# First mixer of a seven-stage transformer kernel: three pieces of the norm per weight tile, the rotation's addition in halves, the maxima of heads 8 to 15 scaled on ScalarE

## The chip, the cores and the metric

The kernel runs on one core of a Trainium2 chip. The metric is device time in microseconds (us) of one execution, as a median over runs. The core has five engines that run their own instruction lists and meet by semaphores: TensorE (PE; its weight loads are PEld), VectorE (DVE), ScalarE (ACT), GpSimd (POOL) and SyncE (SP), which issues the weight loads from memory.

## The reference, cut to what matters

The input has 256 rows of 1024 columns. The program is a chain of seven stages: a feed-forward (`f1`), an attention mixer (`m1`), `f2`, a second mixer (`ab`), `f3`, a third (`cd`), `f4`. All of it is in float32. Only `m1` matters here:

```python
h = _rmsnorm(x, mix_pre_g[l])
qkv = h @ w_qkv[l]
qa, ka, va, qb, kb, vb = jnp.split(qkv, QKV_SPLITS, axis=-1)
qa = _rmsnorm(qa.reshape(B, S, N_HEADS_A, HEAD_DIM), q_norm_g[l])
ka = _rmsnorm(ka.reshape(B, S, N_KV_A, HEAD_DIM), k_norm_g[l])
...
qa = _apply_axial_rope(qa, ang_row, ang_col)
ka = _apply_axial_rope(ka, ang_row, ang_col)
out_a = _gqa_dense_blocked(qa, ka, va)
qb = _apply_rope(qb.reshape(B, S, N_HEADS_B, HEAD_DIM), ang_1d)
kb = _apply_rope(kb.reshape(B, S, N_HEADS_B, HEAD_DIM), ang_1d)
out_b = _dilated_mixture(qb, kb, vb)
heads = jnp.concatenate([out_a.reshape(B, S, A_Q), out_b.reshape(B, S, B_QKV)], axis=-1)
x = x + _rmsnorm(heads @ w_out[l], mix_post_g[l])
```

Heads 0 to 7 (group a) have a norm per head and dense attention over 256 keys; heads 8 to 15 (group b) have a mask (`c_maskb`, which adds up the three dilated patterns) and no norm. Each head is a softmax of 256 x 256 logits.

## The kernel before

Every float32 matmul operand is split into a high and a low part, and a product takes three matmuls (`mm3`). Weights stream in tiles of 128 x 1024: SP loads `wraw`, ACT casts it to the high part `wh` (line 89), DVE (in a few places POOL) subtracts to get the low part `wl` (line 94). There are 4 raw and 6 split buffers; a tile is split about six tiles ahead of its use.

In `m1` the projections come first. `gemm_a` (line 559) takes four weight tiles; after each it runs `self.pump(2)`, that is two small functions from the list `self.bg`, and then perhaps a function of `between`. The first `gemm_a` has in `self.bg` the nine pieces of `rope_a` (norm and rotation: the queries of rows 128 to 255, then the two keys' halves); the second transposes the rotated heads (`tr`, line 810) and runs `step(0)`; the third has the eight pieces of `rope_b` (rotation of the group-b queries and keys) in `self.bg`, and runs `step(1)` to `step(4)` after its four tiles. Then `step(5)` to `step(19)` follow without a projection.

A step is a slot of a software pipeline over the 16 heads, written out in this order: `logits(i)` (six matmuls `lg`, then row maxima `mx` on DVE, for heads 8 to 15 by two instructions of line 848 that add the mask as well, then the scaling of `mx` by -0.125 at line 850), `soft(i-1)` (two exponentials on ACT with `mx` as bias, a reciprocal on DVE at line 859, a product on POOL at line 860), in even steps `pair` (ACT and DVE write out two heads), `trans(i-3)` (four transposes `pT`, ACT's cast to `pp` at line 870, DVE's subtraction for the low part of `pp` at line 871), `pv_(i-4)` (six matmuls `o`, of which the last two read the low part of `pp`). From step 16 on, a piece of the output projection (`wo`) stands in the place of the logits. The tiles `t3` of the rotation and `pp` of the steps come from the same two buffers (tag `pp`).

Nothing is scheduled by a compiler: each engine's list has the order in which the code was written, and an engine takes its list from the front.

Of the kernel before, what the change touches and what calls it, by code (L numbers as in the profile page):

```python
# [11 lines left out]
AF = mybir.ActivationFunctionType  # L12
ALU = mybir.AluOpType
# [175 lines left out]
class Kern:  # L189
# [366 lines left out]
            self.pump(1)  # L556
        return pv

    def gemm_a(self, between=None):

        bank = [self.ps("ga0"), self.ps("ga1")]
        for i in range(4):
            wh, wl = self.ws.take(1)[0]
            for h in range(2):
                t = slice(h * P, (h + 1) * P)
                prods = [((self.xh[:, 2 * i + k, t], self.xl[:, 2 * i + k, t]), (wh[:, k, :], wl[:, k, :]))
                         for k in range(2)]
                self.mm3(bank[h], prods, i == 0, i == 3)
            self.pump(2)
            if between and i in between:  # L570
                between[i]()
        return bank
# [148 lines left out]
    def mixer1(self, gnext):  # L721
        nc, A = self.nc, self.A
        tt = nc.vector.tensor_tensor
        with ExitStack() as st:
# [8 lines left out]
            rb = T([P, 2, 16, 64], "rb")  # L733
# [5 lines left out]
                out=fl(qa[:, h, 0:8, :]), in_=self.gemm_a_half(h, mid, sf)))  # L739
# [47 lines left out]
            def rope_b(h):  # L787
                w = {}

                def a():  # L790
                    w["t"] = ap.tile([P, 16, 64], F32, name="t3", tag="pp", bufs=2)
                    tt(out=rb[:, h], in0=qb[:, h], in1=rope[:, h, 2:3, :].to_broadcast([P, 16, 64]), op=ALU.mult)

                def b(y):
                    a, b = slice(32 * y, 32 * y + 32), slice(32 - 32 * y, 64 - 32 * y)
                    tt(out=w["t"][:, :, a], in0=qb[:, h, :, b],
                       in1=rope[:, h, 3:4, a].to_broadcast([P, 16, 32]), op=ALU.mult)

                def c():
                    tt(out=rb[:, h], in0=rb[:, h], in1=w["t"], op=ALU.add)  # L800

                return [a, lambda: b(0), lambda: b(1), c]

            def tr(src, dst, chunks):

                for c in chunks:
                    p = self.ps("tq")
                    for j, cc in enumerate(c):
                        for h in range(2):
                            nc.tensor.transpose(p[:, j * S + h * P:j * S + (h + 1) * P],  # L810
                                                src[:, h, cc * P:(cc + 1) * P], self.ident)
                    n = len(c)
                    pv = p[:, :n * S].rearrange("p (a t) -> p a t", a=n)
                    hi, lo = (t[:, c[0]:c[-1] + 1:max(1, c[-1] - c[0]), :] for t in dst)
                    nc.scalar.copy(out=hi, in_=pv)
                    tt(out=lo, in0=pv, in1=hi.bitcast(F32), op=ALU.subtract)
# [10 lines left out]
            def logits(i):  # L827
                p = self.ps("lg")
                pv = p.rearrange("p (h k) -> p h k", h=2)
                if i < 8:  # L830
                    o = 64 * (i // 4)
                    q, k = [t[o:o + 64, i % 4, :] for t in qta], [t[o:o + 64, 4, :] for t in qta]
                else:
                    n = i - 8
                    o = 64 * (n % 2)
                    q, k = [t[o:o + 64, n // 2, :] for t in qtb], [t[o:o + 64, 4 + n // 2, :] for t in qtb]
                for h in range(2):
                    t = slice(h * P, (h + 1) * P)
                    self.mm3(pv[:, h, :], [((q[0][:, t], q[1][:, t]), k)], True, True)
                mx = self.sm.tile([P, 2], F32, name="mx", tag="mx")  # L840
                e = ap.tile([P, 2, S], F32, name="e", tag="e")
                if i < 8:
                    src = pv
                    nc.vector.tensor_reduce(out=mx, in_=pv, axis=AX.X, op=ALU.max)
                else:
                    src = e
                    for h in range(2):
                        nc.vector.tensor_tensor_reduce(out=src[:, h, :], in0=pv[:, h, :], in1=mask[:, h, :], scale=1.0,
                                                       scalar=-3e38, op0=ALU.add, op1=ALU.max, accum_out=mx[:, h:h + 1])
                nc.vector.tensor_scalar(out=mx, in0=mx, scalar1=-0.125, scalar2=None, op0=ALU.mult)  # L850
                lg[i] = src, e, mx

            def soft(i):
                src, e, nm = lg[i]
                l = self.sm.tile([P, 2], F32, name="ls", tag="ls")
                for h in range(2):
                    nc.scalar.activation(out=e[:, h, :], in_=src[:, h, :], func=AF.Exp, bias=nm[:, h:h + 1], scale=0.125,
                                         accum_out=l[:, h:h + 1])
                nc.vector.reciprocal(out=l, in_=l)
                nc.gpsimd.tensor_tensor(out=e, in0=e, in1=l.rearrange("p (h o) -> p h o", o=1).to_broadcast([P, 2, S]),  # L860
                                        op=ALU.mult)

            def trans(i):
                e = lg.pop(i)[1]
                p = self.ps("pT")
                for k in range(2):
                    for h in range(2):
                        nc.tensor.transpose(p[:, k * S + h * P:k * S + (h + 1) * P], e[:, h, k * P:(k + 1) * P], self.ident)
                t = ap.tile([P, 2, 512], F32R, name="pp", tag="pp", bufs=2)
                nc.scalar.copy(out=t[:, 0, :], in_=p)  # L870
                tt(out=t[:, 1, :], in0=p, in1=t[:, 0, :].bitcast(F32), op=ALU.subtract)
                pt[i] = t

            def pv_(i):
                pp = pt.pop(i).rearrange("p x (k q) -> p x k q", k=2)
                c = i // 2
                if i % 2 == 0:
                    od[c] = self.ps("o")[:, 0:256]
                o = od[c]
                prods = []  # L880
                for k in range(2):
                    o1 = 2 * (i // 4) + 1 - i % 2 if i < 8 else i % 2
                    v = [(t[:, k] if i < 8 else t[:, k, c - 4])[:, o1:o1 + 2, :].rearrange("p a w -> p (a w)")
                         for t in (va if i < 8 else vb)]
                    prods.append((v, (pp[:, 0, k, :], pp[:, 1, k, :])))
                ops = [(v[0], p[0]) for v, p in prods] + [(v[1], p[0]) for v, p in prods] + [(v[0], p[1]) for v, p in prods]
                for n, (v, p) in enumerate(ops):
                    nc.tensor.matmul(out=o, lhsT=v, rhs=p, start=i % 2 == 0 and n == 0, stop=i % 2 == 1 and n == 5)  # L888

            def pair(c):  # L890
                o = od.pop(c)
                hi, lo = heads(c)
                nc.scalar.copy(out=hi, in_=o)
                tt(out=lo, in0=o, in1=hi.bitcast(F32), op=ALU.subtract)
# [12 lines left out]
            def step(i):  # L907
                if i < 16:
                    logits(i)
                else:  # L910
                    wout(i - 16, 0)
                if 1 <= i < 17:
                    soft(i - 1)
                if i >= 6 and i % 2 == 0:
                    pair((i - 6) // 2)
                if 3 <= i < 19:
                    trans(i - 3)
                if i >= 4:
                    pv_(i - 4)
                if i == 5:  # L920
                    qtb.extend([mp.tile([P, 8, S], F32R, name="qtbh", tag="qb"), mp.tile([P, 8, S], F32R, name="qtbl")])
                if 5 <= i < 9:
                    tr(rbf, qtb, ((i - 5, i - 1),))
                if i in (8, 10, 12, 14):
                    self.ws.copy_next()(nc.gpsimd)


            bank = self.gemm_a()
            for h in range(2):
                nc.scalar.copy(out=fl(qb[:, h, 0:8, :]), in_=bank[h])  # L930
            self.flush()
            bank = self.gemm_a({1: lambda: tr(raf, qta, ((4,), (0, 1))), 2: lambda: tr(raf, qta, ((2, 3),)), 3: lambda: step(0)})
            for h in range(2):
                nc.scalar.copy(out=fl(qb[:, h, 8:16, :]), in_=bank[h])
            self.bg += rope_b(0) + rope_b(1)
            bank = self.gemm_a({i: lambda i=i: step(i + 1) for i in range(4)})
            self.ws.used()
            for h in range(2):
                hi, lo = (t[:, h, :, 0:3:2, :] for t in vb)
# [831 lines left out]
```

## Time and profile before

| | us |
|---|---|
| median of 3 runs (1093.35 to 1094.99) | 1094.9 |
| the profiled execution | 1095.59 |
| its span, first to last instruction | 1093.8 |
| PE busy in the span | 1077.5 (99%) |
| DVE busy | 737.9 (67%) |
| ACT busy | 597.6 (55%) |
| POOL busy | 314.9 (29%) |

The span is what the trace shows, 1.8 us less than the execution's time. Matmuls are pipelined, so a PE that is busy by the table may still be short of its peak. Shares are means over stages with different limits.

### The profile page before, as it was taken

The numbers are of one execution on the slowest core, as the hardware profiler recorded it, in microseconds if no ns is written. First come the engines' busy times: TensorE is split into PE (matmuls) and PEld (weight loads), VectorE is DVE, ScalarE is ACT, GpSimd is POOL, SyncE is SP. The second block draws the span as 40 slices with busy tenths as digits, with TensorE's granted clock in tenths as the row PEclk, the third lists the DMA queues.
The fourth block names the chain that finished last, engine by engine and source line by source line (L and its number), as shares of the span: only waits on it lengthen the run. The fifth ranks groups of instructions, "written<-read, shape, count | busy, mean of one in ns | idle before, by whom it ended". The sixth has DMA issues, their size and how long they took to land.

```text
span 1093.8 us, 16124 instructions
## 1 busy us (share of the span) xinstructions
PE 1077.5 (99%) x5963; PEld 921.9 (84%) x5963; DVE 737.9 (67%) x1023; ACT 597.6 (55%) x952; POOL 314.9 (29%) x564
## 2 busy tenths in 40 slices
PE   8999999999999999999999999999999999999997
PEld 5888888878878888888988888888889888888886
DVE  5665676889676655657775676766778567565564
ACT  4567555556656555556576554554553465554553
POOL 4005840213310000004014699999406100000000
PEclk9999999999999999999999999999999999999999
DMA  7765665672057555655624665565554346656651
GB/s 249 244 209 174 194 209 175 184 220 78 20 158 228 196 190 192 195 190 174 216 77 132 208 198 174 168 200 186 162 177 159 96 135 204 201 171 203 203 171 61
DMA packets 130256, 190.83 MB, mean 174 GB/s; under 512 B 6017, under 2 KB 101249, under 8 KB 130178
## 3 DMA queue, kind: packets, MB, share of 16 engines
q1 hardware_dynamic: 129440, 187.72, 53.7%
q0 software_dynamic: 736, 2.08, 0.7%
q8 instruction: 47, 0.77, 0.3%
q14 instruction: 31, 0.25, 0.1%
q10 hardware_dynamic: 2, 0.00, 0.0%
HBM read 188.73 MB, written 1.05 MB: 174 GB/s over the span
## 4 chain that ended last, share of the span: by engine, by line
PE 89%; DVE 5%; ACT 1%; issue 1%; POOL 1%; DMA 1%; SPq 0%; POOLq 0%; DVEq 0%; ACTq 0%
PE gb L535 27%; PE f L523 21%; PE gb L537 13%; PE wo L523 5%; PE gb L523 5%; PE fh L642 4%; PE gh L523 3%; PE ga L523 2%; DVE wl L94 1%; PE tp L370 1%; PE lg L523 1%; PE o L888 1%; PE M L1392 1%; DMA wraw<-in_w_first_dram 1%; DMA wraw<-in_w_qkv_dram 1%
## 5 line engine op out<-in xcount | busy, mean ns | idle before, releaser
L94 DVE TENSOR_TENSOR wl<-wraw,wh 128x1024 fp32r<-128x1024 f32 x338 | 411.5, 1258 | 107.1 <-ACT wh L89 106.0
L535 PE MATMUL gb<-xt,wh 128*128 128x512 f32 x1280 | 439.3, 390 | 0.0
L89 ACT CAST wh<-wraw 128x1024 fp32r<-128x1024 f32 x340 | 344.8, 1049 | 54.3 <-PE f L523 11.0
L537 PE MATMUL gb<-xt,wl 128*128 128x256 f32 x1280 | 354.0, 277 | 0.0
L535 PEld LDWEIGHTS gb<-xt,wh 128*128 128x128 f32 x1280 | 240.3, 188 | 50.5
L537 PEld LDWEIGHTS gb<-xt,wl 128*128 128x128 f32 x1280 | 240.4, 188 | 1.8
L523 PE MATMUL f<-wh,hh 128*128 128x512 f32 x348 | 138.2, 397 | 0.0
L523 PE MATMUL f<-wh,hl 128*128 128x512 f32 x348 | 137.2, 394 | 0.0
L523 PE MATMUL f<-wl,hh 128*128 128x512 f32 x348 | 136.9, 393 | 0.0
L659 ACT COPY sg<-gb 128x256 f32<-128x256 f32 x80 | 29.9, 374 | 141.3 <-PE gb L537 141.2
L660 DVE TENSOR_TENSOR sg<-gb,sg 128x256 f32<-128x256 f32 x80 | 33.3, 423 | 91.7 <-ACT sg L659 91.3
L344 POOL TENSOR_TENSOR v<-ss 128x1 f32<-128x1 f32 x22 | 6.6, 298 | 289.3 <-ACT xs L336 180.8
L523 PEld LDWEIGHTS f<-wh,hl 128*128 128x128 f32 x348 | 65.3, 188 | 16.9 <-DVE hl L654 0.9
L523 PEld LDWEIGHTS f<-wh,hh 128*128 128x128 f32 x348 | 65.4, 188 | 14.6
L523 PEld LDWEIGHTS f<-wl,hh 128*128 128x128 f32 x348 | 65.4, 188 | 13.2
L339 POOL TENSOR_SCALAR ss<-ss 128x1 f32<-128x1 f32 x6 | 2.4, 398 | 234.2 <-ACT xs L336 234.2
L523 PE MATMUL gb<-xt,wh 128*128 128x256 f32 x384 | 69.5, 283 | 0.0
L659 ACT COPY su<-gb 128x256 f32<-128x256 f32 x80 | 29.2, 366 | 66.9 <-PE gb L537 66.9
L523 PEld LDWEIGHTS gb<-xt,wh 128*128 128x128 f32 x384 | 59.4, 188 | 0.3
L523 PE MATMUL gb<-xt,wl 128*128 128x256 f32 x192 | 54.2, 283 | 0.0
L523 PE MATMUL wo<-wh,xt 128*128 128x512 f32 x160 | 52.5, 399 | 0.0
L653 ACT CAST hh<-sg 128x512 fp32r<-128x512 f32 x40 | 24.9, 623 | 50.4 <-DVE sg L680 50.4
(405 smaller groups left out, 1595.6 us busy)
## 6 DMA issues: line engine op xcount, KB each, us to landing
wraw<-in_ffn_w_down_dram SPq DMA_DIRECT2D x88, 512.0 KB, 3.7
wraw<-in_ffn_w_gate_dram SPq DMA_DIRECT2D x80, 512.0 KB, 4.2
wraw<-in_ffn_w_up_dram SPq DMA_DIRECT2D x80, 512.0 KB, 5.4
wraw<-in_ab_w_in_dram SPq DMA_DIRECT2D x20, 512.0 KB, 4.1
wraw<-in_w_qkv_dram SPq DMA_DIRECT2D x18, 512.0 KB, 3.8
wraw<-in_w_first_dram SPq DMA_DIRECT2D x16, 512.0 KB, 4.3
wraw<-in_cd_w_in_dram SPq DMA_DIRECT2D x16, 512.0 KB, 4.1
wraw<-in_w_out_dram SPq DMA_DIRECT2D x8, 512.0 KB, 3.5
```

What stands on the lines that cost most here:

```text
L89: self.nc.scalar.copy(out=h, in_=r)
L94: eng.tensor_tensor(out=l, in0=r, in1=h.bitcast(F32), op=ALU.subtract)
L370: nc.tensor.transpose(p[:, j * P:(j + 1) * P], src[:, (b + j) * P:(b + j + 1) * P], self.ident)
L523: self.nc.tensor.matmul(out=out, lhsT=l, rhs=r, start=start and i == 0, stop=stop and i == n - 1)
L535: self.nc.tensor.matmul(out=p, lhsT=wh[:, k % 4, c], rhs=self.x2[:, k, :], start=k == 0, stop=False, skip_group_check=True)
L537: self.nc.tensor.matmul(out=p[:, S:2 * S], lhsT=wl[:, k % 4, c], rhs=self.xh[:, k, :], start=False, stop=k == 7, skip_group_check=True)
L642: nc.tensor.matmul(out=p, lhsT=l, rhs=r, start=n == 0, stop=n == 23)
L653: nc.scalar.copy(out=hh, in_=t)
L659: nc.scalar.copy(out=t[:, c, :], in_=p[:, 1, :])
L660: tt(out=t[:, c, :], in0=p[:, 0, :], in1=t[:, c, :], op=ALU.add)
L888: nc.tensor.matmul(out=o, lhsT=v, rhs=p, start=i % 2 == 0 and n == 0, stop=i % 2 == 1 and n == 5)
L1392: nc.tensor.matmul(out=pv[:, a, :], lhsT=l, rhs=F[:, a, 0:4, :].rearrange("p s q -> p (s q)"), start=r == 0, stop=r == 1)
```

## The change

It has three parts, all in `m1`. (1) `gemm_a` gets an argument `pieces`, and the first call runs three pieces of `rope_a` after each tile instead of two. (2) The last piece of `rope_b`, one addition over 16 heads, becomes two over 8 heads each; `rope_b` then has ten pieces instead of eight, of which eight run in the third `gemm_a` as before, and a `self.flush()` behind it runs the other two. (3) For heads 8 to 15 the scaling of `mx` becomes an activation (Copy with scale -0.125) on ACT.

```diff
-    def gemm_a(self, between=None):
+    def gemm_a(self, between=None, pieces=2):
...
-            self.pump(2)
+            self.pump(pieces)
...
-                def c():
-                    tt(out=rb[:, h], in0=rb[:, h], in1=w["t"], op=ALU.add)
-
-                return [a, lambda: b(0), lambda: b(1), c]
+                def c(y):
+                    n = slice(8 * y, 8 * y + 8)
+                    tt(out=rb[:, h, n], in0=rb[:, h, n], in1=w["t"][:, n], op=ALU.add)
+
+                return [a, lambda: b(0), lambda: b(1), lambda: c(0), lambda: c(1)]
...
-                nc.vector.tensor_scalar(out=mx, in0=mx, scalar1=-0.125, scalar2=None, op0=ALU.mult)
+                if i < 8:
+                    nc.vector.tensor_scalar(out=mx, in0=mx, scalar1=-0.125, scalar2=None, op0=ALU.mult)
+                else:
+                    nc.scalar.activation(out=mx, in_=mx, func=AF.Copy, scale=-0.125)
...
-            bank = self.gemm_a()
+            bank = self.gemm_a(pieces=3)
...
             bank = self.gemm_a({i: lambda i=i: step(i + 1) for i in range(4)})
+            self.flush()
```

ACT's list in steps 10 and 11 before (numbers tell tiles apart: `mx_2774` and `e_2775` are those of head 9, `mx_2805` and `e_2806` of head 10; `pp_2822` and `pp_2854` of heads 7 and 8):

```order
L857 ACTIVATE e_2775,ls_2810<-e_2775,mx_2774 128x256 x2
L893 CAST hah_2657<-o_2747 128x256
L870 CAST pp_2822<-pT_2817 128x512
L857 ACTIVATE e_2806,ls_2844<-e_2806,mx_2805 128x256 x2
L870 CAST pp_2854<-pT_2849 128x512
```

The same steps of ACT's list now (`mx_2807` is that of head 10, `mx_2841` that of head 11, `e_2777` that of head 9, `pp_2824` that of head 7):

```order
L854 ACTIVATE mx_2807<-mx_2807 128x2
L861 ACTIVATE e_2777,ls_2812<-e_2777,mx_2776 128x256 x2
L897 CAST hah_2659<-o_2749 128x256
L874 CAST pp_2824<-pT_2819 128x512
L854 ACTIVATE mx_2841<-mx_2841 128x2
L861 ACTIVATE e_2808,ls_2846<-e_2808,mx_2807 128x256 x2
```

In each step the scaling of head i's maxima now stands ahead of the exponentials of head i-1 and of the cast for head i-3.

DVE's list now, from the maxima of head 10 to those of head 11:

```order
L849 ISA e_2808,mx_2807<-lg_2800,maskb_134 128x256
L849 ISA mx_2807 128x1
L863 RECIPROCAL ls_2812<-ls_2812 128x2
L898 TENSOR_TENSOR hal_2660<-o_2749,hah_2659 128x256
L875 TENSOR_TENSOR pp_2824<-pT_2819,pp_2824 128x512
L849 ISA e_2842,mx_2841<-lg_2834,maskb_134 128x256
```

Only the scaling went from this list (it stood ahead of the reciprocal); the maxima of head 11 stand behind the low part of `pp` of head 7, as before.

DVE's list around step 4 before (`rb` is the rotated tile, `mx_2573` and `pp_2587` are those of step 4, `vbl` the low part of the values):

```order
L796 TENSOR_TENSOR t3_2519<-qb_1942,rope_132 128x16x32
L800 TENSOR_TENSOR rb_1944<-rb_1944,t3_2519 128x1024
L844 TENSOR_REDUCE mx_2573<-lg_2566 128x2
L850 TENSOR_SCALAR mx_2573<-mx_2573 128x2
L859 RECIPROCAL ls_2577<-ls_2577 128x2
L871 TENSOR_TENSOR pp_2587<-pT_2582,pp_2587 128x512
L942 TENSOR_TENSOR vbl_140<-ga0_2426,vbh_139 128x4x2x64
```

And now:

```order
L796 TENSOR_TENSOR t3_2520<-qb_1942,rope_132 128x16x32 x2
L845 TENSOR_REDUCE mx_2573<-lg_2566 128x2
L852 TENSOR_SCALAR mx_2573<-mx_2573 128x2
L863 RECIPROCAL ls_2577<-ls_2577 128x2
L875 TENSOR_TENSOR pp_2587<-pT_2582,pp_2587 128x512
L801 TENSOR_TENSOR rb_1944<-rb_1944,t3_2520 128x512 x2
L947 TENSOR_TENSOR vbl_140<-ga0_2426,vbh_139 128x4x2x64
```

The last addition of the rotation went from ahead of step 4's work to behind it, in two halves.

## Rows read from the trace of the kernel before

**Rows 1.** The page's first part: busy time, share of the span, instructions.

```profile
PE 1077.5 (99%) x5963; PEld 921.9 (84%) x5963; DVE 737.9 (67%) x1023; ACT 597.6 (55%) x952; POOL 314.9 (29%) x564
```

**Rows 2.** PE's waits: who waited for whom, us in total, times, longest.

```profile
PE o L888 <- DVE pp L871: 1.2, 2, 0.7
...
PE tq L810 <- DVE ra L773: 0.9, 1, 0.9
```

**Rows 3.** PE's timeline: start, us, instruction, in brackets the idle time before it.

```profile
235.39 0.77 PE L810 MATMUL tq<-ident,ra 128*128 128x128 f32 x5 [0.87 <-DVE ra L773]
...
262.79 0.50 PE L888 MATMUL o<-pp,vah 128*128 128x256 f32 x2 [0.56 <-DVE pp L871]
...
276.49 0.50 PE L888 MATMUL o<-pp,vah 128*128 128x256 f32 x2 [0.66 <-DVE pp L871]
...
287.60 0.40 PE L888 MATMUL o<-pp,vbh 128*128 128x256 f32 x2
287.84 0.40 PE L523 MATMUL wo<-wh,hah 128*128 128x512 f32 x1
...
289.22 0.60 PE L868 MATMUL pT<-ident,e 128*128 128x128 f32 x4
289.58 0.48 PE L888 MATMUL o<-pp,vbh 128*128 128x256 f32 x2
```

**Rows 4.** DVE's timeline in steps 8 to 15.

```profile
270.36 0.41 DVE L848 CUSTOM_DVE_ANT_0 e<-lg,maskb 128x256 f32<-128x256 f32 x1
...
273.73 2.05 DVE L850 TENSOR_SCALAR mx<-mx 128x2 f32<-128x2 f32 x1
...
276.36 0.41 DVE L848 CUSTOM_DVE_ANT_0 e<-lg,maskb 128x256 f32<-128x256 f32 x1
...
277.04 0.08 DVE L848 DVE_READ_ACCUMULATOR2_ANT mx<- 128x1 f32 x1
...
277.74 0.69 DVE L871 TENSOR_TENSOR pp<-pT,pp 128x512 fp32r<-128x512 f32 x1
278.35 0.41 DVE L848 CUSTOM_DVE_ANT_0 e<-lg,maskb 128x256 f32<-128x256 f32 x1
...
286.85 0.42 DVE L848 CUSTOM_DVE_ANT_0 e<-lg,maskb 128x256 f32<-128x256 f32 x1 [0.24 <-PE lg L523]
```

**Rows 5.** ACT's timeline in step 10.

```profile
275.88 0.51 ACT L857 ACTIVATE e<-e,mx 128x256 f32<-128x256 f32 x1 [1.18 <-DVE ls L859]
...
276.88 0.35 ACT L893 CAST hah<-o 128x256 fp32r<-128x256 f32 x1
277.13 0.58 ACT L870 CAST pp<-pT 128x512 fp32r<-128x512 f32 x1
```

**Rows 6.** POOL's timeline, in step 9 and in the third mixer.

```profile
273.31 2.44 POOL L94 TENSOR_TENSOR wl<-wraw,wh 128x1024 fp32r<-128x1024 f32 x1 [0.70 <-ACT wh L89]
...
859.12 1.30 POOL L1452 TENSOR_TENSOR st<-sz,sinT 128x512 f32<-128x512 f32 x1
```

**Rows 7.** DVE's timeline, a reciprocal of the third mixer.

```profile
860.30 0.17 DVE L1487 RECIPROCAL ld<-ld 128x2 f32<-128x2 f32 x1 [1.12 <-ACT ed L1484]
```

**Rows 8.** ACT's groups by form: count, busy us, mean ns of one, idle before.

```profile
L1484 ACT ACTIVATE ed<-ed,mxd 128x128 f32<-128x128 f32 x4 | 1.6, 404 | 17.8 <-DVE mxd L1482 17.8
...
L963 ACT ACTIVATE e<-z 128x4 f32<-128x4 f32 x1 | 0.2, 207 | 0.0
```

**Rows 9.** Stretches: us, busy of each engine, granted clock, DMA share, GB/s.

```profile
258.00:270.00 12.00, 11.44 (x84) 9.93 (x84) 11.83 (x25) 8.52 (x26) 4.06 (x5) 1.00 0.17 46
270.00:288.00 18.00, 17.34 (x127) 15.22 (x127) 16.37 (x61) 14.77 (x47) 10.18 (x9) 1.00 0.08 30
```

**Rows 10.** DVE's timeline: the last norm piece, and around step 4.

```profile
232.21 1.22 DVE L94 TENSOR_TENSOR wl<-wraw,wh 128x1024 fp32r<-128x1024 f32 x1
...
235.04 0.29 DVE L773 TENSOR_TENSOR ra<-t,rra 128x128 f32<-128x128 f32 x1 [0.28 <-POOL rra L757]
...
260.05 1.23 DVE L800 TENSOR_TENSOR rb<-rb,t 128x1024 f32<-128x1024 f32 x1
...
262.06 0.67 DVE L871 TENSOR_TENSOR pp<-pT,pp 128x512 fp32r<-128x512 f32 x1
```

## The prediction, made before the changed kernel had run

> **What bounds the kernel now.** I read first the page's busy times: TensorE works in 99% of the span [rows 1]. So a change that touches no matmul can win only what TensorE waits for. Second, TensorE's waits: among them stand two small entries of the first mixer, the heads' low part (`o` behind `pp`, 1.2 us in two waits) and one transpose behind the norm (0.9) [rows 2]. Third, the timeline, which shows the three places: A, 0.87 us at 235.39, where `tq` waits for the norm's last piece; B, 0.56 at 262.79, and C, 0.66 at 276.49, where `o` waits for the low part of `pp` [rows 3]. Together 2.09 us. That is the most that the change can take away. The work after the mixer has TensorE as its bound, so I pass every microsecond that TensorE loses or wins in the mixer on to the end, one for one.
>
> Fourth, what is late at each place. A: VectorE splits a weight tile at 232.21 (1.22 us), and the norm's last piece begins at 235.04 and lasts 0.29, after 0.28 of waiting for GpSimd [rows 10]. B: the rotation's addition of 1.23 us at 260.05 stands ahead of the low part at 262.06 [rows 10]. C: the scaling of two numbers at line 850 took 2.05 us at 273.73 [rows 4]; a weight split on GpSimd ran from 273.31 to 275.75 [rows 6], and the scaling ended at 275.78, together with it.
>
> Fifth, VectorE and ScalarE in steps 8 to 15. From 270 to 288 VectorE is busy 16.37 of 18 us and ScalarE 14.77 [rows 9]; so there is little slack in either, and the order of their lists counts.
>
> **The change, part by part.**
>
> *Three pieces per tile (A).* The norm's pieces come earlier, and the third weight split no longer stands ahead of the last one. But that piece waited for GpSimd already (0.28), and its forerunners now come sooner than GpSimd's roots. I take 0.4 of the 0.87 as won; bounds nothing and 0.87.
>
> *The addition in halves (B).* It now stands behind step 4's work, so that wait of 0.56 goes. Two things become late in its place: the transposes of `rb`, which open step 5 (263.13 in the old order, right behind that `o`), now wait for the halves; and `t3` outlives step 4, and holds one of the two `pp` buffers while the steps want both, so the cast for head 2 must wait for head 1's `o`. No row shows either. The nearest price for each is that of the addition and a low part standing in line, 0.6 each at most half covered; for A and B together I take 0: bounds −1.0 (all of B and some of A kept) and +0.3 (both new waits in full).
>
> *The scaling on ScalarE.* What goes from VectorE: eight instructions of about 0.17 us, and the hold of 2 us at C. What comes to ScalarE: eight small activations. Their price alone: a 128x4 activation lasts 207 ns [rows 8], and activations and casts overlap (a cast of 0.35 us at 276.88, the next at 277.13 [rows 5], so 0.10 of it is hidden): 0.11 us each. Bounds 0.08 (the read of an accumulator [rows 4]) and 0.30 (a 128x128 activation of 404 ns [rows 8], less the same 0.10).
>
> That is not what decides. The place in the list does. Before, ScalarE in step i needed only what VectorE had scaled in step i−1, and could run while VectorE took the new maxima. Now its first work in step i is the scaling of maxima(i), and behind it in the same list stand the exponentials of head i−1 and the cast for head i−3. VectorE's next maxima stand behind the low part of head i−3, which needs that cast. So the engines hand one token round a ring, once per step, with nothing beside it:
>
> 1. maxima(i), first to last accumulator: 276.36 to 277.12 [rows 4] = 0.76;
> 2. VectorE to ScalarE: 273.73 + 2.05 = 275.78 [rows 4] to 275.88 [rows 5] = 0.10;
> 3. the scaling = 0.11;
> 4. two exponentials: 275.88 to 276.88 [rows 5] = 1.00;
> 5. in even steps the cast `hah`: 276.88 to 277.13 [rows 5] = 0.25;
> 6. the cast to `pp`, until VectorE's low part starts: 277.13 [rows 5] to 277.74 [rows 4] = 0.61;
> 7. the low part, until the next maxima: 277.74 to 278.35 [rows 4] = 0.61.
>
> An odd step takes 3.19, an even one 3.44. TensorE's own step is much shorter: from the middle `o` at 276.49 to the closing one at 287.60 [rows 3] there are five steps, 2.2 us each. So in steps 8 to 15 the ring is the bound, and TensorE waits about 1.1 us per step, at the `o` that reads the low part.
>
> The clock of the ring starts at the maxima of head 8, 270.36 [rows 4] (with A and B at 0). Step 8 still has one 128x512 cast for the rotated heads (0.58, as the cast in [rows 5]) in it: head 9 at 270.36 + 3.44 + 0.58 = 274.38; then 277.57, 281.01, 284.20, 287.64, 290.83, and head 15 at 294.27. It stood at 286.85 [rows 4]: +7.42. C is inside this sum: VectorE is no longer held, but its hold has been replaced by the ring.
>
> Now TensorE. The low part of head 11 stands just ahead of those maxima, 293.66 to 294.35. `o` follows 0.06 later (262.06 + 0.67 = 262.73 [rows 10] to 262.79 [rows 3]); its last pair takes 0.24 (287.60 to 287.84 [rows 3]), so the first `wo` starts at 294.65 instead of 287.84: +6.81. In step 16 the `wo` matmuls take 1.38 (287.84 to 289.22) and the transposes 0.36 (to 289.58) [rows 3], so TensorE is at the next `o` at 296.39. The cast for head 12 ends at 294.27 + 0.76 + 0.10 + 0.11 + 1.00 + 0.58 = 296.82, so `o` starts at 296.87: +0.48. Its low part (0.69 behind that) is late by another 0.15. From step 17 there are no maxima left, and TensorE is the bound again; it wins nothing back there, as it had no wait to lose. Sum: 6.81 + 0.48 + 0.15 = 7.4.
>
> *What the Trainium skill says of the small activation.* "ScalarE: Activation LUTs", section "What ACT_TABLE_LOAD costs", gives 186 ns plus 0.833 ns a column and half of that hidden behind a neighbour: an estimate of 0.095 instead of 0.11, or 0.1 us less in seven rounds. Its section "Rules for kernel authors" puts a plain multiplication on VectorE, and speaks against this part.
>
> *Held by GpSimd.* That an operation of VectorE can be held is shown by 2.05 us for two numbers. The reciprocal, which now comes first behind the maxima, was not held: 0.17 us at 860.30 [rows 7] inside a GpSimd instruction from 859.12 to 860.42 [rows 6].
>
> **The rivals.**
>
> R1, the other side: the ring does not bind. It would not if its seven links came to less than TensorE's 2.2, or if the scaling let the exponentials pass. Then VectorE is relieved and only the waits go: 0.4 + 0.3 + 0.66 = 1.4, thus 1094.2 for the profiled execution and 1093.5 for the median; with all of 2.09, 1092.8. For it: VectorE is the busier engine [rows 9]. Against it: links 4, 6 and 7 alone are 2.22. Point from which it decides: 2.2 us for the ring. The Trainium skill's "Perfetto Trace Analysis", section "Optimizing Scalar/DVE Operations", is on its side: where VectorE is saturated, moving some work to ScalarE may pay. No row shows the place in the list to be harmless. Chance 0.09.
>
> R2: the reciprocal inherits the hold, and the ring has slack. Then C stays and only A and B win, 0.7 at most: 1094.2. [Rows 7] speak against it. Chance 0.01, and I count it with no change.
>
> R3: the ring binds in part, since ScalarE starts step 8 with a lead, or since two links overlap more than their rows do: 2 to 6 us, some 1097 to 1100.5. Chance 0.08.
>
> R4: TensorE, which would idle a third of these steps, loses its clock. The granted clock is 1.00 in 258 to 288, though TensorE stands still for short times there [rows 9]. At half of it seven steps would take up to 4.4 us, 1.0 more than the ring, and the stretch after it would begin slow: together about 17 more than before, 1112. Chance 0.03.
>
> **How the numbers follow.** The profiled execution of before took 1095.59 (span 1093.8 and 1.8 around it), 0.7 over the median of the runs. 1095.59 + 7.4 + 0 = 1103.0; on the median's scale 1102.3. The likeliest case (0.79) has its own range: −1.0 if A and B are kept, +0.3 if not; the scaling at 0.30 gives seven times 0.19 = +1.3, at 0.08 −0.2: 1101 to 1104. The range to give takes in half of R3 below and a little of unknown handovers above: 1099 to 1104.6. A measurement of this kernel can tell about 0.2% (2.2 us) from no change. Slower by more than that: the likeliest, R4 and most of R3, 0.89. Within it: R1 as priced (1.4 is under 2.2), R2, some of R3, 0.08. Faster: 0.03, since even all of A, B and C (2.09) does not reach the bound.
>
> **What would show it right or wrong in the profile after.** Right: maxima on VectorE 3.2 to 3.45 us apart from head 8 on; ScalarE's new row waiting for VectorE's maxima, more than 1 us each step; TensorE's `o` waiting for `pp` by some 1 us per step; the first `wo` near 294.6; no VectorE instruction of 2 us there. For A: the wait near 235 about half as long; for B: waits of `tq` for `rb` in step 5 and of `o` for head 2. Wrong: maxima still 2.2 apart, or the exponentials starting ahead of the scaling's wait. What would upset it most is an engine that takes work past a waiting instruction, or waits much larger than 0.10 between VectorE and ScalarE.

## The result, and the profile after

The changed kernel took 1104.15 us in the median of four runs (1100.36 to 1105.11), the kernel before 1094.72 (four runs; the 1094.9 of the table above is from three of them); the ratio is 1.008, with a 95% interval from 1.0068 to 1.0093. It is slower, as forecast, and inside the range. The profiled execution took 1103.70 with a span of 1101.9. The mean granted clock differs between the runs: 0.989 in those of 1103.70, 1104.60 and 1105.11, 0.997 in the one of 1100.36. Two more sets of runs of the same kernel, each beside runs of the kernel before, gave 1101.82 (ratio 1.0065, 1.0052 to 1.0077) and 1101.58 (1.0062, 1.0049 to 1.0075); they are under the experiments.

TensorE's busy line says nothing of all this, as matmuls at half clock count as busy:

```profile
PE 1085.6 (99%) x5963; PEld 928.0 (84%) x5963; DVE 736.3 (67%) x1017; ACT 597.6 (54%) x960; POOL 314.3 (29%) x564
```

TensorE's waits and its timeline at the places A, B and C and at the first `wo` ([rows 2, 3] are those of before):

```profile
PE o L892 <- ACT pp L874: 1.0, 1, 1.0
PE o L892 <- DVE pp L875: 0.4, 1, 0.4
PE tq L811 <- DVE ra L773: 0.4, 1, 0.4
...
PE tq L811 <- DVE rb L801: 0.2, 1, 0.2
```

```profile
233.04 0.77 PE L811 MATMUL tq<-ident,ra 128*128 128x128 f32 x5 [0.36 <-DVE ra L773]
260.92 0.33 PE L811 MATMUL tq<-ident,rb 128*128 128x128 f32 x1 [0.17 <-DVE rb L801]
263.58 0.50 PE L892 MATMUL o<-pp,vah 128*128 128x256 f32 x2 [0.38 <-DVE pp L875]
274.90 0.50 PE L892 MATMUL o<-pp,vah 128*128 128x256 f32 x2 [0.97 <-ACT pp L874]
...
295.31 0.63 PE L523 MATMUL wo<-wh,hah 128*128 128x512 f32 x1
```

A fell from 0.87 to 0.36. B (0.56) is gone, and in its place stand the two waits that the prediction named: the transposes of `rb` (0.17) and the `o` for head 2 (0.38). C is gone too; the 0.97 at 274.90 is a new wait, for ScalarE's cast in the ring. From the transposes behind A to the first `wo` there are 62.27 us instead of 52.45. The transposes stand 2.35 us earlier than before; 0.51 of that is A, the other 1.84 was won ahead of the mixer, where the code is the same and the traces differ among themselves: e5 and e12, the same kernel, stand 0.7 us behind this one there. It is put down to the execution and not to the change.

Now the ring. VectorE's timeline (maxima of head 9, the low part in step 9, maxima of heads 10 and 15), then ScalarE's in step 9:

```profile
272.39 0.41 DVE L849 CUSTOM_DVE_ANT_0 e<-lg,maskb 128x256 f32<-128x256 f32 x1
...
273.07 0.08 DVE L849 DVE_READ_ACCUMULATOR2_ANT mx<- 128x1 f32 x1
...
274.88 0.69 DVE L875 TENSOR_TENSOR pp<-pT,pp 128x512 fp32r<-128x512 f32 x1 [0.30 <-ACT pp L874]
275.48 0.42 DVE L849 CUSTOM_DVE_ANT_0 e<-lg,maskb 128x256 f32<-128x256 f32 x1
...
293.34 0.42 DVE L849 CUSTOM_DVE_ANT_0 e<-lg,maskb 128x256 f32<-128x256 f32 x1 [0.44 <-PE lg L523]
```

```profile
273.19 0.20 ACT L854 ACTIVATE mx<-mx 128x2 f32<-128x2 f32 x1 [0.60 <-DVE mx L849]
273.30 0.49 ACT L861 ACTIVATE e<-e,mx 128x256 f32<-128x256 f32 x1
...
274.28 0.56 ACT L874 CAST pp<-pT 128x512 fp32r<-128x512 f32 x1
```

Read it as a round: maxima and handover 0.80 (272.39 to 273.19), scaling 0.11, exponentials 0.98, cast 0.60 (274.28 to 274.88), low part 0.60 (to 275.48), sum 3.09. ScalarE's group for the new line, over steps 8 to 15 (count, busy, mean ns, idle before), shows where the engine waits:

```profile
L854 ACT ACTIVATE mx<-mx 128x2 f32<-128x2 f32 x8 | 1.6, 203 | 12.3 <-DVE mx L849 12.3
```

All its idle time there, 12.3 us, stands ahead of the eight scalings (the slow clock below has its part in it; at full clock, in e5, it is 10.8). The last thing to see is the granted clock (after the busy times), in stretches of the same execution:

```profile
262.00:270.00 8.00, 7.62 (x58) 6.57 (x57) 7.15 (x21) 5.03 (x17) 3.12 (x3) 1.00 0.01 3
270.00:276.00 6.00, 5.03 (x32) 3.76 (x31) 3.85 (x13) 4.24 (x12) 4.38 (x3) 1.00 0.00 0
276.00:286.00 10.00, 10.00 (x43) 8.48 (x42) 5.50 (x21) 5.50 (x20) 3.21 (x4) 0.53 0.18 52
286.00:297.00 11.00, 11.00 (x45) 9.73 (x44) 5.03 (x18) 6.43 (x24) 3.12 (x3) 0.50 0.01 2
297.00:300.00 3.00, 3.00 (x19) 2.60 (x18) 1.12 (x2) 0.64 (x2) 1.04 (x1) 0.98 0.00 0
```

TensorE waited in the first steps of the ring, then its clock fell from 2.4 to 1.2 GHz (granted 0.50) for some 20 us. At that clock TensorE's own step is the longer one, 3.90 us from one set of transposes to the next. Up to head 12 the maxima still keep the ring's distance (3.1 and 3.37 us), as TensorE had time to spare; then they are 3.59, 3.90 and 3.90 apart, and VectorE waits for TensorE (0.44 ahead of head 15's maxima):

```profile
289.22 1.11 PE L872 MATMUL pT<-ident,e 128*128 128x128 f32 x4
...
293.12 1.11 PE L872 MATMUL pT<-ident,e 128*128 128x128 f32 x4
```

So two things lie in this execution, the ring and the clock, and the experiments had to take them apart.

### The profile page after: what moved, and what is told of

Read it like the earlier page. It is cut to its first block, busy times and chain, and to the rows that moved or that the text cites. A ratio compares the mean times of both kernels' runs of the same rounds, so it can differ in the third digit from the quotient of the medians.

```text
span 1101.9 us, 16125 instructions
## 1 busy us (share of the span) xinstructions
PE 1085.6 (99%) x5963; PEld 928.0 (84%) x5963; DVE 736.3 (67%) x1017; ACT 597.6 (54%) x960; POOL 314.3 (29%) x564
## 4 chain that ended last, share of the span: by engine, by line
PE 89%; DVE 5%; ACT 2%; issue 1%; POOL 1%; DMA 1%; SPq 0%; POOLq 0%; DVEq 0%; ACTq 0%
PE gb L535 26%; PE f L523 21%; PE gb L537 13%; PE wo L523 5%; PE gb L523 5%; PE fh L642 4%; PE gh L523 3%; PE ga L523 2%; DVE wl L94 1%; PE o L892 1%; PE tp L370 1%; PE lg L523 1%; PE M L1397 1%; PE pT L872 1%; DMA wraw<-in_w_qkv_dram 1%
## 5 line engine op out<-in xcount | busy, mean ns | idle before, releaser
L89 ACT CAST wh<-wraw 128x1024 fp32r<-128x1024 f32 x340 | 344.4, 1047 | 56.3 <-PE f L523 10.8
```

The costliest lines, as they stand in the source:

```text
L89: self.nc.scalar.copy(out=h, in_=r)
```

## The experiments

For every profiled execution the same four points were read: the transposes behind A, the first maxima of heads 8 and 15, and the first `wo`. "Wait A" is the idle time ahead of the first point. "To head 8" runs from the first point to head 8's maxima, "to head 15" from there to head 15's, "to `wo`" from there on. What a row says of the clock, and its last five columns, belong to the one profiled execution; the median is that of all runs. Times in us:

| kernel | median | ratio to before, interval | wait A | to head 8 | to head 15 | to `wo` | A to `wo` |
|---|---|---|---|---|---|---|---|
| before | 1094.72 | | 0.87 | 34.97 | 16.49 | 0.99 | 52.45 |
| changed, clock fell | 1104.15 | 1.0080, 1.0068 to 1.0093 | 0.36 | 35.45 | 24.85 | 1.97 | 62.27 |
| e5 changed, clock full | 1101.82 | 1.0065, 1.0052 to 1.0077 | 0.37 | 35.45 | 23.29 | 0.48 | 59.22 |
| e12 changed, clock full | 1101.58 | 1.0062, 1.0049 to 1.0075 | 0.35 | 35.46 | 23.30 | 0.48 | 59.24 |
| e1 parts 1, 2 | 1094.93 | 1.0003, 0.9994 to 1.0012 | 0.34 | 35.45 | 16.49 | 0.99 | 52.93 |
| e2 part 3, clock fell for some 10 us | 1102.52 | 1.0076, 1.0061 to 1.0091 | 0.82 | 34.94 | 23.83 | 0.48 | 59.25 |
| e3 scaling last | 1093.61 | 0.9993, 0.9985 to 1.0002 | 0.45 | 35.45 | 15.57 | 0.99 | 52.01 |
| e6 scaling in the middle | 1094.49 | 0.9993, 0.9984 to 1.0002 | 0.56 | 35.47 | 16.80 | 0.49 | 52.76 |
| e7 no scaling | 1093.88 | 0.9989, 0.9980 to 0.9998 | 0.45 | 35.47 | 15.57 | 1.00 | 52.04 |
| e4 filled waits | 1102.17 | 1.0071, 1.0055 to 1.0086 | 0.34 | 35.87 | 23.31 | 0.48 | 59.66 |
| e11 filled waits | 1101.79 | 1.0061, 1.0049 to 1.0074 | 0.35 | 35.88 | 23.34 | 0.47 | 59.69 |
| e8 part 1, scaling last | 1093.65 | 0.9991, 0.9983 to 1.0000 | 0.46 | 34.98 | 15.57 | 1.00 | 51.55 |
| e9 part 1, no scaling | 1092.83 | 0.9983, 0.9974 to 0.9992 | 0.35 | 34.95 | 15.57 | 1.00 | 51.52 |
| e10 e9, rotation earlier | 1092.82 | 0.9987, 0.9977 to 0.9997 | 0.34 | 34.65 | 15.57 | 0.99 | 51.21 |

e1 to e4 ran on one chip (before: 1094.18), e5 to e8 on another (1094.57), e9 to e12 on a third (1094.81); ratios are to the runs of before on the same chip. A ratio is estimated from all runs of both kernels and can differ a little from the quotient of the two medians (most for e6: 0.9993 against 0.9999).

**Which part loses: e1 and e2.** e1 is the changed kernel with the scaling back on VectorE:

```diff
-                if i < 8:
-                    nc.vector.tensor_scalar(out=mx, in0=mx, scalar1=-0.125, scalar2=None, op0=ALU.mult)
-                else:
-                    nc.scalar.activation(out=mx, in_=mx, func=AF.Copy, scale=-0.125)
+                nc.vector.tensor_scalar(out=mx, in0=mx, scalar1=-0.125, scalar2=None, op0=ALU.mult)
```

> Parts 1 and 2 alone; the scaling of heads 8 to 15 is back on VectorE. Ring theory (the loss comes from the place of the scaling in ScalarE's list): no loss, the gain at A (0.87 to 0.36 us in the changed kernel) stays, B gives nothing (0.56 became 0.17 + 0.38), C stays: 0.5 below before, 1094.2. Rival (the re-timed norm and rotation push the mixer into a worse rhythm): 1097 or more. The clock stays at 1.00 from 270 to 300 by the ring theory.

e2 is the kernel before with that edit the other way round, and nothing else.

> Part 3 alone. Ring theory: maxima 3.1 to 3.4 us apart from head 8 on while the clock is full; the time is that of the changed kernel and 0.5 more, 1101 if the clock stays full and 1104.7 if it falls to half. Rival (parts 1 and 2 make the loss): 1094 to 1095.

Parts 1 and 2 lose nothing that can be measured (1.0003), part 3 alone loses as much as all three (1.0076). The clock has its share in e2 as well: three of its four executions have a mean clock of 0.989 to 0.995, and in the profiled one it is at half for some 10 us, of which this stretch holds most:

```profile
276.00:286.00 10.00, 9.37 (x39) 8.24 (x39) 5.31 (x20) 5.57 (x23) 3.90 (x4) 0.55 0.20 52
```

The fourth, with 0.999, took 1101.11, so the loss is there without a fall too. The gain of 0.5 that was expected of e1 did not come: A shrank by 0.53, but the way to head 8's maxima is 0.48 longer, which is part 2. In e1 C is back: VectorE's scaling and GpSimd's weight split, a row of each timeline:

```profile
273.34 2.04 DVE L851 TENSOR_SCALAR mx<-mx 128x2 f32<-128x2 f32 x1
```

```profile
272.92 2.44 POOL L94 TENSOR_TENSOR wl<-wraw,wh 128x1024 fp32r<-128x1024 f32 x1 [0.71 <-ACT wh L89]
```

**The engine or the place in its list: e3, e6 and e7.** e3 takes the activation out of `logits` and writes it behind the cast; e6 puts the same two lines behind `soft(i - 1)`, ahead of the cast.

```diff
                 if 3 <= i < 19:
                     trans(i - 3)
+                if 8 <= i < 16:
+                    nc.scalar.activation(out=lg[i][2], in_=lg[i][2], func=AF.Copy, scale=-0.125)
```

> All three parts, but the scaling on ScalarE is written behind the cast to pp of the same step. ScalarE does the same work, in another order. Ring theory: VectorE's next maxima no longer hang on the scaling; steps of 2.2 us, C gone with the hold of VectorE: 0.5 and 0.7 below before, 1093.5. Rival (eight more activations on a ScalarE that is busy 14.8 of 18 us are the price, in whatever place): 1099 or more.

> All three parts, with the scaling on ScalarE between the exponentials and the cast to pp. Ring theory: the ring is still closed, but without the exponentials: maxima 0.80 with the handover, scaling 0.11, cast 0.60, low part 0.60 = 2.11 in odd steps and 2.36 in even ones (cast hah, if it falls inside), 2.24 in the mean against TensorE's 2.22. So next to no loss against the kernel with the scaling last: 1093.6 to 1094.2. Rival (any wait of ScalarE for VectorE's fresh maxima ahead of the cast costs the same as in the changed kernel): 1099 or more.

e7 has no scaling for these heads:

```diff
-                        nc.vector.tensor_tensor_reduce(out=src[:, h, :], in0=pv[:, h, :], in1=mask[:, h, :], scale=1.0,
-                                                       scalar=-3e38, op0=ALU.add, op1=ALU.max, accum_out=mx[:, h:h + 1])
+                        nc.vector.tensor_tensor_reduce(out=src[:, h, :], in0=pv[:, h, :], in1=mask[:, h, :], scale=-0.125,
+                                                       scalar=3e38, op0=ALU.add, op1=ALU.min, accum_out=mx[:, h:h + 1])
...
-                    nc.scalar.activation(out=e[:, h, :], in_=src[:, h, :], func=AF.Exp, bias=nm[:, h:h + 1], scale=0.125,
+                    nc.scalar.activation(out=e[:, h, :], in_=src[:, h, :], func=AF.Exp, bias=nm[:, h:h + 1], scale=0.125 if i < 8 else -1.0,
```

> Parts 1 and 2, and no scaling for heads 8 to 15 on either engine: the instruction that adds the mask multiplies by -0.125 and takes the minimum, and the exponential takes scale -1. Ring theory: as with the scaling last, no ring, C gone because the reciprocal behind the maxima is not held: 1093.5, within 0.4 of the kernel with the scaling last. Rival on C (the reciprocal inherits the hold): a VectorE instruction of 2 us in step 9 and 1094.2. Rival on the price (eight small activations cost ScalarE's time on the path): 0.9 below the kernel with the scaling last.

ScalarE does the same eight activations in e3 as in the changed kernel, and heads 8 to 15 take 15.57 us instead of 23.29. The place costs everything, the work nothing: without any scaling (e7) it is 15.57 as well. In e6 a shorter ring remains, and it can be read link by link, first on VectorE, then on ScalarE:

```profile
275.76 0.41 DVE L849 CUSTOM_DVE_ANT_0 e<-lg,maskb 128x256 f32<-128x256 f32 x1
...
278.15 0.41 DVE L849 CUSTOM_DVE_ANT_0 e<-lg,maskb 128x256 f32<-128x256 f32 x1
...
279.66 0.69 DVE L873 TENSOR_TENSOR pp<-pT,pp 128x512 fp32r<-128x512 f32 x1 [0.67 <-ACT pp L872]
280.27 0.41 DVE L849 CUSTOM_DVE_ANT_0 e<-lg,maskb 128x256 f32<-128x256 f32 x1
```

```profile
278.95 0.20 ACT L917 ACTIVATE mx<-mx 128x2 f32<-128x2 f32 x1 [0.45 <-DVE mx L849]
279.06 0.57 ACT L872 CAST pp<-pT 128x512 fp32r<-128x512 f32 x1
```

0.80, 0.11, 0.60, 0.61: a round of 2.12, where 2.11 was expected; an even round takes 2.39 (275.76 to 278.15), where 2.36 was. That is about TensorE's step, so hardly anything is lost: by the trace 0.75 against e3, in the medians 1094.49 against e3's 1093.61 on another chip, both at a ratio of 0.9993.

e3 also settles C. The reciprocal is not held by GpSimd's split:

```profile
273.95 0.17 DVE L861 RECIPROCAL ls<-ls 128x2 f32<-128x2 f32 x1 [0.57 <-ACT e L859]
```

```profile
273.00 2.44 POOL L94 TENSOR_TENSOR wl<-wraw,wh 128x1024 fp32r<-128x1024 f32 x1 [0.90 <-ACT wh L89]
```

Without the hold, heads 8 to 15 take 0.92 less than before (16.49 to 15.57); all of it lies in the rounds up to head 12, and the last three take 2.2 us in both.

**The clock: e4, e5, e11 and e12.** e4 and e11 are the changed kernel with the logits' matmuls of heads 8 to 15 done twice:

```diff
-                    self.mm3(pv[:, h, :], [((q[0][:, t], q[1][:, t]), k)], True, True)
+                    for _ in range(1 if i < 8 else 2):
+                        self.mm3(pv[:, h, :], [((q[0][:, t], q[1][:, t]), k)], True, True)
```

> The changed kernel with the logits' matmuls of heads 8 to 15 done twice (the second overwrites the first with the same values), some 0.75 us more TensorE work in each of eight steps, where it waits 0.9 to 1.2. Clock theory (TensorE's waiting in the ring lets its clock fall, and that is a loss of its own, about 3.8 us): clock 1.00 from 270 to 300, the ring's 3.1 to 3.4 us per step stay, and 1100.4 in every run, less than the changed kernel although it does more. Rival (the fall has nothing to do with the waiting): half clock again, steps of 5 us, 1110 or more.

> The changed kernel, unaltered, run many times for its spread, to set beside the one with filled waits (all of whose runs had a mean clock of 0.998 or more). Clock theory: the fall comes in some executions only and by length, so the runs spread over 4 us and more, the long ones with a mean clock of about 0.989 and the short ones with 0.995 and above; median 1102.5 to 1104. Rival (the ring alone sets the time, the clock follows what else happens): a spread of 2 us as in the kernel before, and no relation to the clock.

> The changed kernel with filled waits again, on the same chip and beside the changed kernel. Clock theory: no execution with a mean clock under 0.998; 1101 to 1102.4. Rival (that none of four fell was chance, since only some executions of the changed kernel fall): about half fall, with 0.989 to 0.995.

> The changed kernel again, to set beside the one with filled waits. Clock theory: some executions with a mean clock of 0.989 to 0.995 and 1103 to 1105, the others 1100.4 to 1102 at 0.997 or more; the ring alone 1101.8 as in the executions with the full clock. Rival: all executions alike.

In the profiled execution of e5 the clock did not fall, and the ring stands bare. TensorE's timeline: a wait in a step of the ring, the first `wo`, the `o` of step 16 (0.29 late), the next `wo`:

```profile
278.99 0.51 PE L892 MATMUL o<-pp,vah 128*128 128x256 f32 x2 [0.65 <-ACT pp L874]
...
292.98 0.40 PE L523 MATMUL wo<-wh,hah 128*128 128x512 f32 x1
...
295.01 0.51 PE L892 MATMUL o<-pp,vbh 128*128 128x256 f32 x2
...
296.08 0.40 PE L523 MATMUL wo<-wh,hah 128*128 128x512 f32 x1
```

Its stretches, and one of e4 (the last three figures: clock, DMA share, GB/s):

```profile
270.00:276.00 6.00, 5.03 (x34) 3.87 (x33) 3.13 (x10) 4.95 (x15) 3.66 (x3) 1.00 0.00 0
276.00:286.00 10.00, 8.32 (x52) 6.22 (x50) 5.64 (x21) 5.51 (x20) 3.83 (x4) 1.00 0.17 52
286.00:297.00 11.00, 9.93 (x56) 7.46 (x55) 6.03 (x23) 6.97 (x25) 3.87 (x5) 1.00 0.01 2
```

```profile
276.00:282.00 6.00, 6.00 (x43) 4.96 (x41) 3.04 (x14) 3.58 (x13) 1.93 (x3) 1.00 0.26 87
```

The 14 executions of the changed kernel, sorted, with their mean granted clocks:

```
1100.28  1100.36  1101.17  1101.22  1101.24  1101.58  1101.82  1101.97  1102.58  1103.29  1103.58  1103.70  1104.60  1105.11
 0.998    0.997    0.998    0.998    0.998    0.996    0.999    0.998    0.995    0.993    0.991    0.989    0.989    0.989
```

Eight have 0.996 or more, and their median is 1101.2; six have 0.995 or less, and their median is 1103.6. The line between the two was drawn after the runs were seen. The nine executions with filled waits have 0.998 or 0.999, and take 1100.98 to 1102.35, although TensorE does 48 matmuls more; their ring is the same (23.31 and 23.34). So falls go with TensorE's waiting: 6 of 14 with the waits, none of 9 without. If the fill made no difference, none of 9 would come about by chance in 3 of 100 cases. e2, which has the ring, adds 3 falls of 4, and the seven kernels without the long ring (e1, e3, e6 to e10) have none under 0.997 in 77 executions. Only the executions of 1103.70 (changed) and 1103.12 (e2) were profiled in a fall; in the others it is read from the mean clock.

The size was expected wrong: 1100.4 stood on the one execution of the first four with a full clock, which lies at the low end of such executions (1100.28 to 1101.97). The medians on one chip (1101.79 filled, 1101.58 changed) don't differ, as most executions there kept the clock; for the same reason e5 came out at 1101.82 and not at the 1102.5 to 1104 that were expected. Waiting does not force the fall either: the changed kernel has the same 5.03 us of TensorE's work from 270 to 276 in the execution that fell and in the one that did not.

**A version that beats both: e8, e9 and e10.** e8 is part 1 with e3's place for the scaling, e9 part 1 with e7's edit, both without part 2; e10 is e9 with `pieces=3` in the third `gemm_a` as well.

> Part 1 and the scaling last on ScalarE, without part 2. By the traces part 2 only moved B (0.56 before; 0.17 and 0.38 with it), so the same time as with part 2: 1093.5, within 0.3. Rival (the halves were worth the full 0.56): 0.5 above the kernel with the scaling last; rival (the halves cost): below 1093.

> Part 1 and no scaling for heads 8 to 15, without part 2. In the traces so far part 2 cost 0.47 us between the norm's last wait and head 8's maxima (35.45 against 34.98 us), and the scaling last or not at all was worth the 0.66 of C and about 0.2: so 0.4 below the kernel with all parts and no scaling and 1.3 below before, 1093.2. Rival (that difference is the spread of single executions): the same as with part 2, 1093.8.

> As the kernel before this one, and the rotation's eight pieces run three per weight tile too, so that the addition of 1.23 us stands ahead of step 3's work instead of step 4's. If VectorE has room there: B (0.57) goes, 1092.7. Rival (VectorE, busy 13.76 of 14 us from 244 to 258, hands the delay on to step 3 or to the weight splits): 1093.2 to 1094, with a new wait of TensorE near 256.

Without part 2 head 8's maxima come 0.47 to 0.52 sooner, in both pairs (e3 and e8, e7 and e9). e9 took 1092.83 against 1094.81 on the same chip: 0.9983, an interval from 0.9974 to 0.9992. In e10 B shrinks to a half:

```profile
260.45 0.50 PE L889 MATMUL o<-pp,vah 128*128 128x256 f32 x2 [0.25 <-DVE pp L872]
```

By the trace that is 0.3 us more; the median (1092.82) can't tell it from e9.

## Why the prediction was right, point by point

**The ring** is shown. It forecast links of 0.76, 0.10, 0.11, 1.00, 0.61, 0.61, sum 3.19; measured were 0.80 for the first two, 0.11, 0.98, 0.60, 0.60, sum 3.09. Seven rounds with the cast of step 8 were to take 23.91; they take 23.29 at full clock. The main miss is the handover: 0.10 came from an `e` that waited behind a held VectorE, and it is 0.04 (273.07 + 0.08 = 273.15 to 273.19). That ScalarE would wait for the maxima in each step is shown (10.8 us in all at full clock), that the place in the list decides is shown by e3, and that the eight activations have no price of their own by e7:

```profile
L854 ACT ACTIVATE mx<-mx 128x2 f32<-128x2 f32 x8 | 1.6, 204 | 10.8 <-DVE mx L849 10.8
```

One detail was wrong: TensorE's waits were put at the `o` that reads the low part. In e5 they stand one link earlier, at the first `o`, which reads ScalarE's cast; from 269 to 296 they are 3.7 us in six waits:

```profile
PE o L892 <- ACT pp L874: 3.7, 6, 1.0
```

R3, which had the ring bind in part, for 2 to 6 us, did not come: the first round, in which ScalarE was to have a lead, took 3.90 of the 4.02 of the sum.

**The sum.** For the ring it said 6.81 to the first `wo` and 0.63 behind it, 7.4. At full clock (e5) there are 59.22 − 52.45 − 0.48 (part 2) = 6.29, and 3.10 − 2.54 = 0.56 behind it, where 3.10 is from the first `wo` to the next (292.98 to 296.08) and 2.54 the same from the rows of before (1.38 and 0.36 in [rows 3], then 0.56 for the low part and 0.24 for the last pair). So 6.85, 0.6 less.

**A and B.** The net of 0 is right: A won 0.51 (0.4 forecast), part 2 cost 0.48. The waits named for part 2 are in the trace, and the 0.17 and 0.38 ahead of TensorE's matmuls look like no more than the 0.56 that was saved. But most of the wait for `rb` stands ahead of the weight loads of its transposes, which are rows of PEld:

```profile
260.32 0.20 PEld L811 LDWEIGHTS tq<-ident,rb 128*128 128x128 f32 x2 [0.33 <-DVE rb L801]
260.92 0.14 PEld L811 LDWEIGHTS tq<-ident,rb 128*128 128x128 f32 x1 [0.40 <-DVE rb L801]
```

The whole loss lies between step 4's logits and the second set of transposes, first before, then now:

```profile
260.21 0.38 PE L523 MATMUL lg<-qtah 64*128 64x256 f32 x1
...
265.79 0.60 PE L810 MATMUL tq<-ident,rb 128*128 128x128 f32 x4
```

```profile
257.85 0.38 PE L523 MATMUL lg<-qtah 64*128 64x256 f32 x1
...
263.92 0.60 PE L811 MATMUL tq<-ident,rb 128*128 128x128 f32 x4
```

That is 5.58 and 6.07, so 0.49 more. From start to start, step 4 is 0.82 shorter, as B is gone; the first set of transposes takes 0.70 more, and step 5, with the wait for head 2's `pp`, 0.61 more. So the two new waits together cost more than B did.

**C and R2.** The hold is gone and the reciprocal doesn't inherit it, as was concluded from [rows 6, 7]: 0.17 us inside GpSimd's split in e3. Those rows were weak evidence, as GpSimd's instruction ended 0.12 us after the reciprocal had begun; e3's, with more than 1 us of GpSimd's split still ahead, settles it. The Trainium skill's "SBUF — State Buffer", section "Who interferes with whom", counts tensor_scalar among the operations that can take the port pair shared with GpSimd, and doesn't name the reciprocal; 2.04 us and 0.17 agree with that.

**R1** fell: the ring binds at 3.1 to 3.4 against 2.2. Its price for the vanished waits, 1.4, was too high even where nothing binds: in e3's trace 0.42 is won at A and 0.44 behind it, because part 2 took 0.48 back, and the ratio of 0.9993 can't be told from 1. The Trainium skill's "Perfetto Trace Analysis", section "Optimizing Scalar/DVE Operations", says that moving work from a saturated VectorE to ScalarE may make sense; here the same move cost 6.85 us in one line of the list, and against e1 it gave 0.92 in another (15.57 for 16.49).

**R4** is the step that failed, though the time hid it. It gave a fall of the clock 0.03; it came in 6 of 14 executions, and in the first four, on which the result rests, in three. Its price of 17 us was much too high: it took steps of 4.4 in all seven rounds and a slow stretch behind them. TensorE's step at half clock is 3.90, only the last three rounds became longer by it, and the whole fall costs 62.27 − 59.22 = 3.05 us to the first `wo` and 0.26 behind it (3.36 from the first `wo` to the next, against 3.10).

So the profiled execution's 8.1 us are: −1.84 from ahead of the mixer, −0.51 at A, +0.48 by part 2, 6.85 by the ring, 3.31 by the clock, together 8.29; the 0.2 left over were not looked for. That the median of 1104.15 lies as near to 1102.3 as 1.85 is partly luck: the ring was 0.6 shorter than forecast, and the fall of the clock, which the sum left out, added about 3 us (3.31 by the trace) in three runs of four. Executions at full clock lie at 1101.2, which is inside the range as well.

## What to carry to other kernels

Before an operation is moved to an engine with time to spare, draw what stands behind it in that engine's list and who waits for that: if the way leads back to what the operation itself waits for, one step later, the two engines take turns, and the sum of the round is to be set against the step of the engine that is the bound. Here the operation cost nothing a few lines further down the same list. Where a bound engine begins to wait, read its clock too, in several executions.

## What the runs showed of the hardware that was not expected

TensorE's granted clock fell to half though no wait of its matmuls in the ring was shown longer than 1 us, and it stayed there for some 20 us in which the engine hardly stood still (21.00 us of work in the 21 from 276 to 297), in e2 for some 10; with the same waits it kept its full clock in 8 of 14 executions. What decides between them no run here shows.
